# Gate stores on ScalarE, and one modulation pair with each gate, in a hybrid attention and mLSTM layer

## The chip, the cores and the metric

One Trainium2 chip, one core. The metric is device microseconds of one launch. TensorE is PE in the rows (PEld its weight load), VectorE DVE, ScalarE ACT, GpSimd POOL and SyncE SP. "The granted clock" is the share of TensorE's full 2.4 GHz that the chip granted in a stretch; 0.50 is 1.2 GHz.

## The reference, cut to what matters

One layer over 1,024 prompt rows and 64 sample rows (together T = 1,088 columns, all kept transposed), D_MODEL 1,024.

```python
mod = jax.nn.silu(c) @ w_ada + b_ada              # modulation, 6 x 1024 columns
sh1, sc1, g1, sh2, sc2, g2 = jnp.split(mod[:, None, :], 6, axis=-1)
u = _rmsnorm(x, norm1_g) * (1 + sc1) + sh1
sq, sk, sv, mqk_pre, mv, mo, mi, mf, ga, gb = jnp.split(u @ w_in, idx, axis=-1)
y_a = _stick_breaking(sq, k_all, v_all, q_start)  # 8 heads x 64
y_b = jax.nn.sigmoid(mo) * mlstm(mqk_pre, mv, mi, mf)
merged = jax.nn.sigmoid(ga) * (y_a @ w_a) + jax.nn.sigmoid(gb) * (y_b @ w_b)
x = x + g1 * (merged @ w_out)
u2 = _rmsnorm(x, norm2_g) * (1 + sc2) + sh2
x = x + g2 * ((jax.nn.silu(u2 @ w_ff_gate) * (u2 @ w_ff_up)) @ w_ff_down)
```

Two parts matter here. The gates ga and gb are needed only when the branches are merged, and the modulation from column block 16 on (g1, sh2, sc2, g2) only behind that; so both can be computed at any earlier time, as filling for TensorE.

## The kernel before, in words

Matrix products in f32 are made of three passes in a rounded format: each weight tile (128 columns of a weight matrix, 1,024 rows, 512 KB) is loaded by SP into a buffer `wr`, GpSimd splits it into a high part `wh` (L53) and a low part `wl` (L59), and `mm3` (L76, L77, L78) issues high x high, high x low and low x high. The pool `wp` has three buffers of each kind, used in turn.

The stretch of the program that the change touches has these units.

- A **gate unit** (`gate_unit`, 8 for ga and 8 for gb) loads one weight tile, runs 72 matmuls (3 chunks of 320, 384 and 384 columns, 24 each), takes the sigmoid of each chunk on ACT (L845) into a small tile `gt`, and stores it to a scratch tensor (L846). SP issues that store.
- A **modulation pair** (`ada_unit(i)`, blocks i and i+1; 16 of them are left for this stretch, in `ada_left`) loads two weight tiles `wada` of 512 KB each (L220) into two of the same three `wr` buffers, and has 32 small matmuls on PE (L223) and two transposes (L228).
- A **branch_b** step is one chunk of y_b @ w_b (12 matmuls into `ps_b`), of which there are 24 for 8 blocks and 3 chunks.
- An **attention pair** (`attention(p)`, p = 0 to 3, two heads each, and the sample group's rows) loads q, k and v from scratch by GpSimd (`load_head`, L454 to L457); per query tile PE makes the logits `z` (L546, L547), ACT two sigmoids `re` and `be` (L411, L412), DVE a running product from the right (L415) and a product (L416); then PE transposes (L560), ACT and DVE split the result (L47, L56), and PE multiplies by v (L567).

The fourth mLSTM head is emitted together with the first modulation pair and two gates. Then each of the first three attention pairs is emitted ahead of its filling: `run(attention(p), chain(gates_ada(ng, na)), 27, 0)` with four gates and three or four modulation pairs. The last pair is emitted up to its 14th step, then the filling that is left, then the rest of the pair, and then all of branch_b. What is written first has priority: the framework's scheduler plays the program against its own timeline and writes out a fixed order for each engine, in which work of later text fills the gaps of earlier text. On the chip each engine keeps to that order, and a DMA waits in its engine's queue until its data and its buffer are there. Behind this stretch, from about 900 us on, come w_a, w_out and the FFN.

Of the kernel before, what the change touches and what calls it, by code (L numbers as in the profile page):

```python
# [35 lines left out]
def trunk(ctx, tc, a, o, dbg=None, stop=None):  # L36
    nc = tc.nc
# [126 lines left out]
    def sum_step(x, k, c, when):  # L164

        nc.sync.dma_start(wsum_d[x][0:1, c, HC : HC + 1], when())
        src = sum_parts[x][k]
        src = wsum_d[src][:, c, :] if isinstance(src, int) else wpart(*src, c)
        if k:
            nc.gpsimd.dma_start(wsum_d[x][:, c, :], src, accum_op=ALU.add)  # L170
        else:
            nc.gpsimd.dma_start(wsum_d[x][:, c, :], src)
        return
        yield
# [7 lines left out]
    def small(shape, name, tag, dtype=F32, bufs=2, pool=None):  # L182
        return (pool or cur["sb"]).tile(shape, dtype, tag=tag, name=name, bufs=bufs)
# [170 lines left out]
    def unit(name, fills, evac, alloc=None, last=False):  # L354

        wh, wl = w_unit(fills, name)
        if alloc:
            alloc()
        for c, (s, e) in enumerate(CHUNKS):
            if last and c:  # L360
                break
            ps = bank("d", f"ps_{name}_{c}", cur["d"])
            for kb in range(KB):
                mm3(ps[:, : e - s], wh[:, kb, :], wl[:, kb, :], uh[kb][:, s:e], ul[kb][:, s:e], kb == 0, kb == KB - 1)
            evac(ps, s, e)
            yield
        if last:
            pss = [bank("d", f"ps_{name}_{c}", cur["d"]) for c in (1, 2)]
            for kb in range(KB):
                for ps, (s, e) in zip(pss, CHUNKS[1:]):  # L370
                    mm3(ps[:, : e - s], wh[:, kb, :], wl[:, kb, :], uh[kb][:, s:e], ul[kb][:, s:e], kb == 0, kb == KB - 1)
            for ps, (s, e) in zip(pss, CHUNKS[1:]):
                evac(ps, s, e)
            yield

    def w_cols(c0):
        return lambda raw: [(raw, cols(w_in, c0))]
# [464 lines left out]
    def gate_unit(b, c0, dst, name):  # L842
        def fin(ps, s, e):
            t = small([P, 384], f"gt_{name}{b}_{s}", "gt", bufs=cur["gt"])
            nc.scalar.activation(t[:, : e - s], ps[:, : e - s], AF.Sigmoid)  # L845
            nc.sync.dma_start(dst[b][:, s:e], t[:, : e - s])  # L846
        return unit(f"{name}{b}", w_cols(c0 + b * P), fin, None, name == "gb" and b == KB - 1)

    def in_unit(name, c0, i, evac, alloc):
        return unit(name, w_cols(c0), lambda ps, s, e: evac(*i, ps, s, e), lambda: alloc(*i))  # L850

    def qkv_units(p):
        return [in_unit(f"q{p}", OFF_Q + P * p, (p, 0), evac_qk, alloc_qk),
                in_unit(f"k{p}", OFF_K + P * p, (p, 1), evac_qk, alloc_qk), k_post(p),
                in_unit(f"v{p}", OFF_V + P * p, (p,), evac_v, alloc_v), v_post(p)]

    def ml_units(h):
        return [in_unit(f"mq{h}", OFF_MQ + P * h, (h, 0), evac_x, alloc_x),
                in_unit(f"mk{h}", OFF_MK + P * h, (h, 1), evac_x, alloc_x),
                in_unit(f"mv{h}", OFF_MV + P * h, (h,), evac_mv, alloc_mv),  # L860
                in_unit(f"mo{h}", OFF_MO + P * h, (h,), evac_mo, alloc_mo)]

    def ada_unit(i):

        ada_blocks((i, i + 1), "d", cur["d"], lambda i: wp.tile([P, KB, P], F32, tag="wr", name=f"wada{i}"))
        if i % 8 == 6:
            ada_bias(i - 6, 8)
        if i == 38:
            nc.vector.scalar_tensor_tensor(A2, mod[:, 32:40, :], 1.0, c1T[:, 48:56, None].to_broadcast([P, 8, 2]), ALU.add, ALU.mult)
        yield  # L870

    def chain(gens):
        for g in gens:
            yield from g

    def run(consumer, dense, nsteps, nd):

        n = 0.0
        done = False
        if nd == 0:  # L880
            for _ in consumer:
                pass
            done = True
        for _ in dense:
            n += nsteps / max(nd, 1)
            while n >= 1.0 and not done:
                n -= 1.0
                done = next(consumer, "end") == "end"
        for _ in consumer:
            pass  # L890

    gates = [gate_unit(b, OFF_GA, ga_d, "ga") for b in range(KB)] + [gate_unit(b, OFF_GB, gb_d, "gb") for b in range(KB)]
    ada_left = [ada_unit(i) for i in range(16, 48, 2)]
# [55 lines left out]
    sums = [(x, k, c) for x, k in ((1, 0), (3, 0), (1, 1), (2, 0), (2, 1), (3, 1), (4, 0), (4, 1)) for c in range(2)]  # L949
    for h in range(4):  # L950
        q_, k_, kp, v_, vp = qkv_units(h)
        m_ = ml_units(h + 1) if h < 3 else ada_left[0:1] + gates[0:2]
        def last(t):
            return t[0:1, T - 1 : T]

        said = [None, lambda h=h: last(pairs[h].kf), None, lambda h=h: last(pairs[h].vf), None]
        if h < 3:
            said += [lambda h=h: cvo[0:1, h + 1 : h + 2], lambda h=h: cvo[0:1, h + 5 : h + 6],
                     lambda h=h: last(heads[h + 1].vf), lambda h=h: last(heads[h + 1].og)]
        dense = []  # L960
        for i, g in enumerate([q_, k_, kp, v_, vp] + m_):
            dense.append(g)
            if i < len(said) and said[i] and sums:
                dense.append(sum_step(*sums.pop(0), said[i]))
        run(mlstm(h), chain(dense), 14, 23 if h < 3 else 17)
# [64 lines left out]
                nc.sync.dma_start(pb_d[m][:, s:e], t)  # L1030
                yield

    gi, ai = 2, 1

    def gates_ada(ng, na):
        nonlocal gi, ai
        gs, ads = gates[gi : gi + ng], ada_left[ai : ai + na]
        gi, ai = gi + ng, ai + na
        fill = []
        for i in range(ng):  # L1040
            fill += gs[i : i + 1] + ads[i : i + 1]
        return fill + ads[ng:]

    for p, (ng, na) in enumerate(((4, 3), (4, 4), (4, 4))):
        run(attention(p), chain(gates_ada(ng, na)), 27, 0)

    last_pair = attention(3)
    for _ in range(14):
        next(last_pair)
    for _ in chain(ada_left[ai : ai + 2] + gates[gi : gi + 1] + ada_left[ai + 2 :] + gates[gi + 1 :]):  # L1050
        pass
    wb0 = wide_unit(w_b, 0, 4, 0, "wb0")
    for b in range(4, 8):
# [39 lines left out]
    for m4 in range(0, KB, 4):  # L1093
# [3 lines left out]
        for c, m in [(c, m4 + i) for c in range(3) for i in range(4)]:  # L1097
# [12 lines left out]
            for lo, hi in ([(s, HT), (HT, e)] if s < HT < e else [(s, e)]):  # L1110
                h = lo // HT
# [668 lines left out]
```

## Time and profile before

| what | value |
|---|---|
| runs | 1782.4, 1779.88 and 1782.68 us, median 1782.4 |
| the profiled execution | 1784.58 us, of which its span is 1782.9 us |
| mean granted clock | 0.984 |
| PE busy | 1718.2 us (96%) |
| DVE, ACT, POOL busy | 1030.9, 747.8, 537.1 us (58%, 42%, 30%) |
| first and last gate store | 459.2 and 810.6 us |

The attention pairs lie between about 500 and 898 us. Busy shares are means over stages with different limits, so a change in this stretch is read from windows of it: the idle time of PE in a window, and beside it what PE's work lost by a granted clock under 1 (busy time times what the clock lacks to 1).

### The profile page before, as it was taken

What the parts mean: (1) busy time and instruction counts of PE and PEld (TensorE: products, weight loads), DVE (VectorE), ACT (ScalarE), POOL (GpSimd) and SP (SyncE); (2) the same over time, 40 slices, a digit from 0 to 9 for tenths busy, and PEclk for the clock granted to TensorE, in tenths of its full rate; (3) what the DMA queues carried; (4) which work ended last, traced back from release to release, by engine and by line L of the source; (5) the groups of instructions that cost most, each with busy time, mean ns of one, the idle gap of its engine ahead of it and who ended that gap; (6) DMA issues with size and microseconds to landing.
All of it is one profiled execution on the core that took longest, in us unless ns stands there. A gap on an engine that the chain in (4) does not pass through costs nothing. (4 is left out here: it accounts for less than half of the span.)

```text
span 1782.9 us, 32711 instructions
## 1 busy us (share of the span) xinstructions
PE 1718.2 (96%) x12670; PEld 1658.0 (93%) x12670; DVE 1030.9 (58%) x1962; ACT 747.8 (42%) x1513; POOL 537.1 (30%) x489
## 2 busy tenths in 40 slices
PE   6999999999989999789999999999999999999998
PEld 4899999999979998689899999999999999999998
DVE  5533325152244867576764389766555677667964
ACT  6333333324233535335533457533333345453444
POOL 1434544445433232143567240044322100000000
PEclk9999999999999999899999999999999999999999
DMA  9436666664485666767576355744433588899943
GB/s 274 116 99 209 146 193 143 187 162 138 136 203 150 160 167 151 167 157 244 170 217 191 99 147 166 197 145 166 137 99 98 163 231 240 299 338 356 289 134 101
DMA packets 361838, 320.24 MB, mean 180 GB/s; under 512 B 16983, under 2 KB 330835, under 8 KB 361683
## 3 DMA queue, kind: packets, MB, share of 16 engines
q1 hardware_dynamic: 347378, 270.77, 50.6%
q0 software_dynamic: 14304, 47.39, 10.8%
q8 instruction: 99, 1.62, 0.4%
q14 instruction: 57, 0.46, 0.1%
HBM read 241.01 MB, written 98.09 MB: 190 GB/s over the span
## 5 line engine op out<-in xcount | busy, mean ns | idle before, releaser
L1662 PE MATMUL ps_d<-o,wh_d 128*128 128x272 f32 x1232 | 230.8, 287 | 0.0
L1662 PEld LDWEIGHTS ps_d<-o,wh_d 128*128 128x128 f32 x1232 | 192.8, 188 | 0.0
L1662 PE MATMUL ps_d<-o,wl_d 128*128 128x272 f32 x616 | 176.4, 288 | 0.0
L1662 PEld LDWEIGHTS ps_d<-o,wl_d 128*128 128x128 f32 x616 | 115.5, 188 | 0.0
L47 ACT CAST w<-wr 128x512 fp32r<-128x512 f32 x140 | 84.6, 619 | 68.1 <-DMA wr<-in_w_ff_gate 17.5
L56 DVE TENSOR_TENSOR w<-wr,w 128x512 fp32r<-128x512 f32 x140 | 95.7, 696 | 22.5 <-ACT w L47 20.0
L415 DVE TENSOR_TENSOR_SCAN re<-re 128x128 f32<-128x128 f32 (+3 forms) x64 | 95.4, 1494 | 11.8 <-ACT re L411 11.5
L411 ACT ACTIVATE re<-z 128x512 f32<-128x512 f32 (+2 forms) x96 | 47.6, 496 | 90.3 <-DVE z L407 61.0
L1646 POOL DMA_DIRECT2D dsum_d<-wr_d x12 | 6.5, 538 | 237.4 <-DVE wr_d L1644 232.7
L1435 PE MATMUL ps_ga<-b1h,w 128*128 128x272 f32 x352 | 74.6, 289 | 3.1 <-ACT g L1420 2.0
L1435 PE MATMUL ps_gc<-b5h,w 128*128 128x272 f32 x352 | 75.2, 293 | 0.3 <-DVE g L1423 0.3
L1435 PE MATMUL ps_gd<-b4h,w 128*128 128x272 f32 x352 | 73.9, 290 | 1.3 <-DVE hst L1417 1.3
L1435 PE MATMUL ps_gd<-b7h,w 128*128 128x272 f32 x352 | 74.2, 290 | 0.1
L1435 PE MATMUL ps_gb<-b6h,w 128*128 128x272 f32 x352 | 74.3, 289 | 0.0
L1435 PE MATMUL ps_ga<-b2h,w 128*128 128x272 f32 x352 | 73.8, 288 | 0.0
L1435 PE MATMUL ps_gc<-b3h,w 128*128 128x272 f32 x352 | 73.7, 289 | 0.0
L76 PE MATMUL ps_gb<-uh,wh_gb 128*128 128x384 f32 (+1 forms) x192 | 65.9, 343 | 6.0 <-POOL wh_gb L53 5.2
L47 ACT CAST o<-hr 128x544 fp32r<-128x544 f32 x77 | 49.3, 645 | 51.9 <-DMA hr<-h_d 25.3
L47 ACT CAST wh_d<-wr_d 128x1024 fp32r<-128x1024 f32 (+1 forms) x42 | 41.1, 980 | 69.9 <-PE ps_d L1662 41.0
L76 PE MATMUL ps_ga<-uh,wh_ga 128*128 128x384 f32 (+1 forms) x192 | 65.2, 340 | 2.4 <-POOL wh_ga L53 1.2
L78 PE MATMUL ps_ga<-uh,wl_ga 128*128 128x384 f32 (+1 forms) x192 | 63.9, 333 | 2.6 <-POOL wl_ga L59 2.6
L56 DVE TENSOR_TENSOR o<-hr,o 128x544 fp32r<-128x544 f32 x77 | 53.9, 722 | 20.3 <-ACT o L47 20.0
(560 smaller groups left out, 5840.6 us busy)
## 6 DMA issues: line engine op xcount, KB each, us to landing
wada<-in_w_ada SPq DMA_DIRECT2D x48, 512.0 KB
wr<-wsum_d SPq DMA_DIRECT2D x80, 256.0 KB
wr_d<-in_w_ff_down SPq DMA_DIRECT2D x34, 512.0 KB
h_d<-hst SPq DMA_DIRECT2D x44, 272.0 KB
wr<-in_w_ff_gate SPq DMA_DIRECT2D x40, 256.0 KB
hr<-h_d SPq DMA_DIRECT2D x33, 272.0 KB
wsum_d<-in_w_ff_up POOLq DMA_DIRECT2D x6, 1282.0 KB, 7.7
wsum_d<-in_w_ff_gate POOLq DMA_DIRECT2D x6, 1282.0 KB, 7.9
```

Of the source, the lines that this page charges most:

```text
L47: nc.scalar.copy(out, in_)
L56: nc.vector.tensor_sub(out, in_, h.bitcast(F32))
L76: nc.tensor.matmul(ps, wh, xh, start=first, stop=False)
L78: nc.tensor.matmul(ps, wl, xh, start=False, stop=last)
L411: nc.scalar.activation(rest[:, c0 : c0 + w], ps, AF.Sigmoid, scale=-scale)
L415: nc.vector.tensor_tensor_scan(r, r, r, 1.0, ALU.mult, ALU.bypass)
L1435: nc.tensor.matmul(ps, w[:, a, j, :], b[j // 2][:, j % 2, :], start=p in (1, 6, 5, 7) and j == 0 and k == 0, stop=j == 3 and k == 2, skip_ ...
L1646: nc.gpsimd.dma_start(dsum_d[p][mp, ks[0] // 4][:, : P * n], flat)
L1662: nc.tensor.matmul(ps, a[:, j, mi, :], b[:, h], start=p not in (2, 4) and k == ks[0] and i == 0, stop=k == ks[-1] and i == 2, skip_group_c ...
```

## The change

The gate's store is issued by ACT, right behind the sigmoid whose tile it stores, and no longer by SP. The order of the filling is another: ahead of each gate stands one modulation pair. Before, the sequence on PE is a16 ga0 ga1 | ga2 a18 ga3 a20 ga4 a22 ga5 | ga6 a24 ga7 a26 gb0 a28 gb1 a30 | gb2 a32 gb3 a34 gb4 a36 gb5 a38 | a40 a42 gb6 a44 a46 gb7 (bars where a new attention pair's filling begins in the text); with the change a16 ga0 a18 ga1 | a28 ga2 a20 ga3 a22 ga4 a24 ga5 a26 | ga6 a30 ga7 a32 gb0 a34 gb1 a36 | gb2 a38 gb3 a40 gb4 a42 gb5 a44 | gb6 a46 gb7. All units are the same in number and content.

```diff
--- before.py
+++ after.py
@@ -843,7 +843,8 @@
         def fin(ps, s, e):
             t = small([P, 384], f"gt_{name}{b}_{s}", "gt", bufs=cur["gt"])
             nc.scalar.activation(t[:, : e - s], ps[:, : e - s], AF.Sigmoid)
-            nc.sync.dma_start(dst[b][:, s:e], t[:, : e - s])
+
+            nc.scalar.dma_start(dst[b][:, s:e], t[:, : e - s])
         return unit(f"{name}{b}", w_cols(c0 + b * P), fin, None, name == "gb" and b == KB - 1)
 
     def in_unit(name, c0, i, evac, alloc):
@@ -949,7 +950,7 @@
     sums = [(x, k, c) for x, k in ((1, 0), (3, 0), (1, 1), (2, 0), (2, 1), (3, 1), (4, 0), (4, 1)) for c in range(2)]
     for h in range(4):
         q_, k_, kp, v_, vp = qkv_units(h)
-        m_ = ml_units(h + 1) if h < 3 else ada_left[0:1] + gates[0:2]
+        m_ = ml_units(h + 1) if h < 3 else [ada_left[0], gates[0], ada_left[1], gates[1]]
         def last(t):
             return t[0:1, T - 1 : T]
 
@@ -1030,24 +1031,24 @@
                 nc.sync.dma_start(pb_d[m][:, s:e], t)
                 yield
 
-    gi, ai = 2, 1
+    gi, ai = 2, 2
 
     def gates_ada(ng, na):
         nonlocal gi, ai
         gs, ads = gates[gi : gi + ng], ada_left[ai : ai + na]
         gi, ai = gi + ng, ai + na
-        fill = []
-        for i in range(ng):
-            fill += gs[i : i + 1] + ads[i : i + 1]
-        return fill + ads[ng:]
-
-    for p, (ng, na) in enumerate(((4, 3), (4, 4), (4, 4))):
+        fill = ads[ng:]
+        for g, ad in zip(gs, ads):
+            fill += [g, ad]
+        return fill
+
+    for p, (ng, na) in enumerate(((4, 5), (4, 4), (4, 4))):
         run(attention(p), chain(gates_ada(ng, na)), 27, 0)
 
     last_pair = attention(3)
     for _ in range(14):
         next(last_pair)
-    for _ in chain(ada_left[ai : ai + 2] + gates[gi : gi + 1] + ada_left[ai + 2 :] + gates[gi + 1 :]):
+    for _ in chain([gates[gi], ada_left[ai], gates[gi + 1]]):
         pass
     wb0 = wide_unit(w_b, 0, 4, 0, "wb0")
     for b in range(4, 8):
```
The change has one line more in `gate_unit` (an empty one), so its line numbers behind it are higher by one: the store is L847.

Three places of the program show what it moves. The first is **SP's queue ahead of the last attention pair's filling**, with the modulation loads (`wada`, the number is the block) and the gates' loads (`wr_gb`). Before:

```order
L220 DMA wada39_8025<-in_w_ada 128x8x128
L220 DMA wada40_8398<-in_w_ada 128x8x128
L846 DMA gb_d_97<-gt_gb5_0_7955 128x320
L846 DMA gb_d_97<-gt_gb5_320_7983 128x384
L846 DMA gb_d_97<-gt_gb5_704_8011 128x384
L220 DMA wada41_8408<-in_w_ada 128x8x128
L220 DMA wada42_8424<-in_w_ada 128x8x128
L220 DMA wada43_8434<-in_w_ada 128x8x128
L467 DMA craw_v3_8065<-in_cache_sb_v 128x4x128
L64 DMA wr_gb6_8449<-in_w_in 128x8x128
L220 DMA wada44_8540<-in_w_ada 128x8x128
```
With the change:

```order
L220 DMA wada42_7979<-in_w_ada 128x8x128
L220 DMA wada43_7989<-in_w_ada 128x8x128
L64 DMA wr_gb5_8004<-in_w_in 128x8x128
L220 DMA wada44_8095<-in_w_ada 128x8x128
L585 DMA ya_d_94<-ya1_6006 128x1088
L220 DMA wada45_8105<-in_w_ada 128x8x128
L64 DMA wr_gb6_8475<-in_w_in 128x8x128
L220 DMA wada46_8566<-in_w_ada 128x8x128
L220 DMA wada47_8576<-in_w_ada 128x8x128
L64 DMA wr_gb7_8592<-in_w_in 128x8x128
```
Before, three modulation loads stand in a row behind the stores, and three more behind the load for gb6; with the change two loads and one gate's load alternate, and no gate store stands between them.

The second is **GpSimd's order at the start of the first attention pair**: the splits of gates 2 and 3, the fourth mLSTM head's output (`ybs`) and the loads of the first head (`qs`, `kh`, `kl`). Before:

```order
L53 TENSOR_SCALAR wh_ga3_5578<-wr_ga3_5576 128x1024
L59 TENSOR_TENSOR wl_ga3_5579<-wr_ga3_5576,wh_ga3_5578 128x1024
L812 TENSOR_TENSOR hsq3_4708<-hn3_4191 128x1152
L53 TENSOR_SCALAR ybs3_0_4770<-yb3_4754 128x1088
L59 TENSOR_TENSOR ybs3_1_4773<-yb3_4754,ybs3_0_4770 128x1088
L454 DMA qs0_0_4854<-qk_d_178 64x1088
L455 DMA kh0_0_4855<-qk_d_178 64x1088
L456 DMA kl0_0_4856<-qk_d_178 64x1088
```
With the change:

```order
L53 TENSOR_SCALAR wh_ga2_5514<-wr_ga2_5512 128x1024
L59 TENSOR_TENSOR wl_ga2_5515<-wr_ga2_5512,wh_ga2_5514 128x1024
L53 TENSOR_SCALAR ybs3_0_4762<-yb3_4746 128x1088
L59 TENSOR_TENSOR ybs3_1_4765<-yb3_4746,ybs3_0_4762 128x1088
L53 TENSOR_SCALAR wh_ga3_5630<-wr_ga3_5628 128x1024
L59 TENSOR_TENSOR wl_ga3_5631<-wr_ga3_5628,wh_ga3_5630 128x1024
L454 DMA qs0_0_4880<-qk_d_178 64x1088
L455 DMA kh0_0_4881<-qk_d_178 64x1088
L456 DMA kl0_0_4882<-qk_d_178 64x1088
```
Gate 3's two splits stood ahead of `ybs`; they now stand between `ybs` and the first head's loads.

The third is **PE's order at the start of the last head's long chain** (`z3_1_6` and `z3_1_7` are the logits of the last two query tiles; that head takes its tiles from the back). Before:

```order
L499 MATMUL z0s3_8339<-ckl3_8330,zq_4852 128x512
L546 MATMUL z3_1_6_512_8709<-kh3_1_8054,qs3_1_8053 128x384
L547 MATMUL z3_1_6_512_8709<-kl3_1_8055,qs3_1_8053 128x384
L76 MATMUL ps_b4_1_9332<-yh4_8688,wh_wb4_9236 128x384
L77 MATMUL ps_b4_1_9332<-yl4_8689,wh_wb4_9236 128x384
L78 MATMUL ps_b4_1_9332<-yh4_8688,wl_wb4_9237 128x384
L76 MATMUL ps_b4_1_9332<-yh5_8690,wh_wb4_9236 128x384
```
With the change:

```order
L546 MATMUL z3_1_6_0_8706<-kh3_1_8132,qs3_1_8131 128x512
L547 MATMUL z3_1_6_0_8706<-kl3_1_8133,qs3_1_8131 128x512
L77 MATMUL ps_b7_2_9465<-yl7_8695,wh_wb6_9242 128x384
L78 MATMUL ps_b7_2_9465<-yh7_8694,wl_wb6_9243 128x384
L546 MATMUL z3_1_6_512_8709<-kh3_1_8132,qs3_1_8131 128x384
L547 MATMUL z3_1_6_512_8709<-kl3_1_8133,qs3_1_8131 128x384
L506 MATMUL ps_as3_8439<-ident_66,be_s3_8430 128x128 x4
L509 MATMUL ps_as23_8448<-ident_66,be_s3_8430 64x128
L546 MATMUL z3_1_7_0_8722<-kh3_1_8132,qs3_1_8131 128x512
L547 MATMUL z3_1_7_0_8722<-kl3_1_8133,qs3_1_8131 128x512
```
Before, branch_b's steps `ps_b4_1` to `ps_b7_1` and `ps_b4_2` to `ps_b7_2` stand behind `z3_1_6_512`, between the steps of the chain; with the change all of branch_b stands ahead of it.

## Rows read from the trace of the kernel before

**Rows 1.** Page, part 1: engine, busy time, share of the span, instructions.

```profile
PE 1718.2 (96%) x12670; PEld 1658.0 (93%) x12670; DVE 1030.9 (58%) x1962; ACT 747.8 (42%) x1513; POOL 537.1 (30%) x489
```

**Rows 2.** Windows (start:end | length, busy us and instructions per engine, granted clock, DMA share, GB/s).

```profile
560.00:735.00 175.00, 171.75 (x1297) 158.40 (x1297) 121.26 (x221) 83.86 (x193) 46.89 (x52) 1.00 0.61 155
735.00:740.00 5.00, 2.22 (x30) 1.89 (x30) 1.07 (x5) 1.52 (x3) 0.58 (x1) 1.00 0.97 269
740.00:760.00 20.00, 12.44 (x77) 8.44 (x66) 9.90 (x28) 5.05 (x13) 7.08 (x8) 0.50 0.92 188
760.00:780.00 20.00, 20.00 (x162) 18.15 (x160) 11.99 (x20) 8.32 (x21) 3.01 (x4) 0.99 0.41 116
780.00:800.00 20.00, 15.34 (x101) 13.75 (x100) 19.89 (x26) 6.83 (x17) 15.89 (x12) 0.91 0.88 210
```

**Rows 3.** Timeline of PE, 735 to 763 us (start, length, engine, line, operation [idle before <- releaser]).

```profile
739.72 0.77 PE L223 MATMUL ps_ada<-wada,cT 128*32 128x128 f32 x16 [2.78 <-DMA wada<-in_w_ada]
...
745.78 1.08 PE L223 MATMUL ps_ada<-wada,cT 128*32 128x128 f32 x16 [2.36 <-DMA wada<-in_w_ada]
...
756.38 0.63 PE L76 MATMUL ps_gb<-uh,wh_gb 128*128 128x320 f32 x1 [4.65 <-POOL wh_gb L53]
```

**Rows 4.** Timeline of SP's queue, 712 to 760 us.

```profile
722.66 9.81 SPq L846 DMA_DIRECT2D gb_d<-gt_gb  x3
734.33 3.52 SPq L220 DMA_DIRECT2D wada<-in_w_ada  x3
...
743.48 15.69 SPq L220 DMA_DIRECT2D wada<-in_w_ada  x3
```

**Rows 5.** Waits of SP's queue, whole span: who is waited for, us in total, times, longest.

```profile
SPq L846 <- ACT gt_gb L845: 88.1, 21, 8.2
...
SPq L846 <- ACT gt_ga L845: 53.3, 15, 6.5
```

**Rows 6.** Line 846: instructions of it (ns min/median/max, first and last start).

```profile
L846 SPq DMA_DIRECT2D gb_d<-gt_gb x24: 319/338/339, 609.3 to 810.6; - x24
```

**Rows 7.** Windows, around the start of the first attention pair.

```profile
480.00:560.00 80.00, 73.96 (x522) 68.36 (x521) 35.72 (x69) 26.26 (x58) 31.56 (x31) 0.96 0.71 169
515.00:520.00 5.00, 2.62 (x23) 1.31 (x20) 2.78 (x6) 1.53 (x4) 2.78 (x3) 0.82 0.29 92
520.00:525.00 5.00, 3.15 (x12) 3.16 (x13) 1.67 (x3) 0.66 (x2) 1.79 (x1) 0.50 0.68 206
```

**Rows 8.** Timeline of POOL, 483 to 503 us.

```profile
487.88 0.60 POOL L454 DMA_DIRECT2D qs<-qk_d  x1
```

**Rows 9.** DMA issues, 485 to 505 us: xcount, KB each, median us to landing.

```profile
kl<-qk_d POOLq DMA_DIRECT2D x4, 272.0 KB, 11.6
```

**Rows 10.** Timeline of PE, 497 to 503 us.

```profile
500.98 0.40 PE L546 MATMUL z<-kh,qs 128*128 128x128 f32 x2
```

**Rows 11.** Timeline of POOL, 514 to 545 us.

```profile
519.46 2.33 POOL L59 TENSOR_TENSOR wl_ga<-wr_ga,wh_ga 128x1024 fp32r<-128x1024 f32 x1
...
539.11 1.05 POOL L53 TENSOR_SCALAR wh_ga<-wr_ga 128x1024 fp32r<-128x1024 f32 x1 [4.09 <-DMA wr_ga<-in_w_in]
```

**Rows 12.** Windows, the fill ahead of the last head's chain, and that chain.

```profile
820.00:855.00 35.00, 33.71 (x220) 32.56 (x219) 16.34 (x25) 18.35 (x39) 18.05 (x16) 1.00 0.60 192
855.70:897.70 42.00, 37.70 (x221) 34.08 (x221) 37.49 (x57) 24.60 (x57) 24.80 (x20) 0.96 0.51 164
882.00:897.70 15.70, 12.70 (x85) 10.42 (x84) 13.71 (x27) 10.29 (x24) 7.58 (x11) 1.00 0.66 219
```

**Rows 13.** Timeline of PE, 854 to 862 us.

```profile
855.93 0.33 PE L77 MATMUL ps_b<-yl,wh_wb 128*128 128x384 f32 x1
...
857.67 0.33 PE L78 MATMUL ps_b<-yh,wl_wb 128*128 128x384 f32 x1
```

**Rows 14.** Timeline of DVE, 855 to 900 us.

```profile
855.97 0.30 DVE L407 TENSOR_TENSOR z<-z,amask 128x128 f32<-128x128 f32 x1 [6.13 <-PE z L547]
...
897.77 0.62 DVE L56 TENSOR_TENSOR yl<-ya,yh 128x320 fp32r<-128x320 f32 x1 [0.53 <-ACT yh L47]
```

## The prediction

> **What bounds the kernel now.** I read the page's engine shares first: PE is busy 96% of the span [rows 1], so a change pays only where it fills a hole of PE or gives its clock back. The windows come next, because the mean hides where the holes are. From 560 to 735 us, where gates and modulation pairs alternate one for one, PE is idle 175.00 − 171.75 = 3.25 us at full clock, 1.9% [rows 2]. In the next 65 us, where the last pairs stand bunched (a38, a40, a42, then one gate, then a44, a46), idle time is 2.78 + 7.56 + 0 + 4.66 = 15.0 us, and the granted clock falls to 0.50 for 20 us and to 0.91 for another 20: busy time times the missing clock is 12.44 × 0.50 + 20.00 × 0.01 + 15.34 × 0.09 = 7.8 us [rows 2]. That is 22.8 us lost in 65. The timeline of PE names what it waited for: twice a modulation load, then the split of gate gb6's weights [rows 3]. SP's timeline shows those loads one behind the other, the last three drawn out over 15.69 us, with stores that held the queue for 9.81 us ahead of them [rows 4], and the DMA engines are over 0.9 busy for the 25 us from 735 us on [rows 2]. A pair brings 1 MB for some 2 us of PE work; bunched, it starves PE, spread it does not.
>
> **The change, part by part.**
>
> *1. The bunch is dissolved (gain).* The same 65 us at the rate of the stretch before would lose 65 × 1.9% = 1.2 us, so 22.8 − 1.2 = **−21.6 us**. Upper end: all of it, −22.8. Lower end: 780 to 800 us has DVE busy 19.89 of 20 us [rows 2], so its loss of 4.66 + 1.4 = 6.1 us may be the attention chain's own, which leaves −15.5. I take −21.6, because DVE was held up by the starved PE just before (9.90 of 20 us busy) and was catching up.
>
> *2. The first attention pair starts later (cost).* Gate 3's load now stands on SP behind wada21, whose buffer comes free only when PE has done pair a28, and its splits stand on GpSimd ahead of the first head's loads. Those loads began at 487.88 us [rows 8], they take a median of 11.6 us from issue to landing [rows 9], and the first logits ran at 500.98 [rows 10]: 13.1 us from the first load to the first logits, nearly all of it loading. With the change a28 comes right behind gate 1 and the mLSTM's last transposes, at about 487 us as I count PE's order; three weight tiles then queue, of which one alone took 4.09 us from free buffer to landed [rows 11]. I put gate 3's at 493, its splits (1.05 + 2.33 us, [rows 11]) at 497, the head loads at 498, the first logits at 498 + 13 = 511 us. PE arrives there at about 500 (487 plus gate 2's 72 matmuls of 0.17 us), so it stands for about 10 us; the matmuls behind run at half clock for a few us, as they did behind the stall at 520 us [rows 7], 2.5 us; and 0.5 more for what follows. That is 13 us. What the stretch loses now goes with it: 480 to 560 us has 6.04 us idle and 2.62 × 0.18 + 3.15 × 0.50 = 2.1 us of clock [rows 7], 8.1 in all, most of it waits on splits that moved ahead. Net **+4.9 us**. Ends: −2 (the head loads hide behind gate 2 and half of today's waits go) and +13 (both stay).
>
> *3. The last head's chain loses its cover (cost).* In the trace PE works on branch_b while the last head's chain goes through ACT and DVE. DVE waited 6.13 us for PE's logits at 855.97 and ends at 898.4 [rows 14]; until then PE set the time, with 33.71 of 35 us busy [rows 12]. Behind these logits stand 8 steps of branch_b, 8 × 12 = 96 matmuls at (857.67 − 855.93) / 10 = 0.174 us [rows 13], 16.7 us. The change puts them all ahead of the logits: PE reaches them **+16.7 us** later. The chain behind is then freed of them. It took 42.0 us with DVE busy 37.49 and PE 37.70 [rows 12]; PE keeps 37.7 − 16.7 = 21.0 us, so DVE's own 37.5 us is the bound: **−4.5 us**. Ends for the bare chain: 32 us (the sample rows' scan and product move ahead, and GpSimd's 24.80 us of products, which ran beside DVE, mostly too) and 50 us (rival B). Net +12.2.
>
> *4. The stores change queue.* SP's queue waited 88.1 + 53.3 = 141 us for sigmoids [rows 5]; that goes. It pays nothing by itself, since PE was idle only 3.25 us in the 175 us with the most of these waits; this is the end on the side of gain, −3.3. ACT issues 48 stores more, 48 × 0.338 = 16.2 us [rows 6], over some 350 us in which it was busy 83.86 of 175, or 48% [rows 2]. A store waits for nothing on ACT but the sigmoid just ahead. Queued behind it are the next sigmoids of attention, and DVE waits for those; if that cover were gone, a fifth of the 16.2 us would show, +3. I take **0**. The Trainium skill (DMA: Bandwidth & Descriptors, "Issuing engines are not separate DMA queues") says that DMAs issued by different engines run on the same 16 DMA engines, and that spreading them saves only the issue time. By it the end of −3.3 falls away and the sum stays.
>
> w_a, w_out and the FFN stay as they are: 0.
>
> Sum: −21.6 + 4.9 + 12.2 + 0 = **−4.5 us**. The sum is made against the profiled execution, 1784.58 us, which gives 1780.1. That execution lies 2.2 us above the median of the runs, so against 1782.4 the forecast is **1777.9 us**. No measurement of this kernel can tell less than about 0.2%, 3.6 us, from no change.
>
> **The rivals.**
>
> *A, no measurable change.* The loss only moves: the stall at the first pair takes its upper end of +13, or the gain its lower end of −15.5, while the chain costs its +12.2. The first gives −21.6 + 13 + 12.2 = +3.6, the second −15.5 + 4.9 + 12.2 = +1.6; both with some luck elsewhere lie within 3.6 us of zero: about 1782. For it: the bytes and the matmuls are the same. Against it: the bunch is the largest hole of the stretch.
>
> *B, slower: the bare chain lasts longer.* Without branch_b, PE has 21.0 us of work in the chain in many short pieces between waits on ACT and DVE. In the trace the granted clock was 0.50 where PE was busy 12.44 of 20 us with small pieces [rows 2], and 1.00 where it was busy 12.70 of 15.7 at the chain's end [rows 12]. If the clock falls, PE's part takes up to 42 us and stands in series with ACT and DVE. The point from which it decides is a chain of 42.0 + 4.5 − 0.9 = 45.6 us: there the sum becomes −21.6 + 4.9 + 16.7 + 3.6 = +3.6. At 50 us it is +8.0, **1790 us**. The Trainium skill (TensorE: Matmul & The Clock Gate, Part 1) states that the throttled state is the default and that activity releases it; by that rule the sparse chain falls to 1.2 GHz. The two stretches named show one of each.
>
> *C, a larger gain.* The chain shrinks to 32 us and the start costs nothing: −21.6 − 2 + 16.7 − 10 = −16.9, **1765.5 us**. For it: DVE's work shares its time with GpSimd's products now. Against it: PE, ACT and DVE wait for each other in the chain.
>
> *D, the change does only the stores' part*, if the order on the chip were not what moves the time: 0 from part 4, inside A.
>
> **How the numbers follow.** Forecast, between −3.6 and −10 us: 0.38. A with D: 0.28. B, with the start's stall at its upper end counted in: 0.24. C and what lies between it and the forecast: 0.10. Faster is then 0.38 + 0.10 = 0.48, the same 0.28, slower 0.24. For 8 in 10 the range takes in most of C and of B: **1766 to 1790 us**; the likeliest case's own range is 1772 to 1779.
>
> **What would show it.** Step 1: the windows of the stretch that holds gb5 to gb7 show PE over 97% busy at a clock of 1.00, and no wait on `wada` above 1 us. Step 2: PE waits about 10 us for the first head's loads near 500 us; without that wait the step is wrong. Step 3: no `ps_b` matmul behind `z3_1_6_512`, and 37 to 38 us from there to the last `yl`; the granted clock in it tells B. Step 4: no store of gates on SP, and DVE's waits on ACT's `re` no longer than before. The forecast is wrong if new waits on `wada` appear where a28 was pulled ahead, or if the chain is over 45.6 us.

## The result and the profile after

The changed kernel takes 1791.93 us in the median of four runs (1790.43 to 1794.98), the kernel before 1782.54 us. The ratio is 1.0057, 95% interval [1.004, 1.0075], that is +10.2 us (7.1 to 13.4). It is slower, above the range of 1766 to 1790, where 4.5 us less was forecast. The profiled execution, the longest of the four, has a span of 1793.3 us against 1782.9 us before.

The windows of the changed kernel, cut at the same places of the program as far as that is possible (columns as in [rows 2]; 870.08 us is the last head's `z3_1_6_512`, 906.93 us the end of the last `yl`):

```profile
480.00:560.00 80.00, 69.61 (x514) 64.40 (x513) 36.20 (x70) 23.43 (x53) 29.48 (x31) 0.91 0.76 188
560.00:735.00 175.00, 169.66 (x1254) 154.82 (x1253) 119.62 (x219) 80.31 (x187) 55.04 (x54) 0.99 0.64 159
735.00:800.00 65.00, 62.21 (x441) 58.92 (x440) 40.11 (x64) 27.11 (x63) 27.56 (x23) 0.97 0.68 203
800.00:870.00 70.00, 65.01 (x405) 62.05 (x404) 41.95 (x67) 35.78 (x79) 36.25 (x32) 0.98 0.67 182
870.08:906.93 36.85, 25.57 (x129) 19.25 (x129) 34.19 (x60) 20.14 (x48) 22.70 (x20) 0.81 0.30 99
```

Idle time of PE plus what its work lost by a clock under 1 (here and below summed over windows of 5 us, since a mean clock over a long window also counts idle time). The last row is different: it gives the length of that part, with the 96 matmuls at the prediction's 16.7 us. In the kernel before it begins at 855.52 us, where this row is `z3_1_6_512`:

```profile
855.52 0.34 PE L547 MATMUL z<-kl,qs 128*128 128x384 f32 x1
```

| stretch | before | changed | difference | forecast |
|---|---|---|---|---|
| 480 to 560 us | 8.1 | 10.4 + 4.6 = 15.0 | +6.9 | +4.9 |
| 560 to 735 us | 3.3 | 5.3 + 1.4 = 6.7 | +3.4 | 0 |
| 735 to 800 us | 22.8 | 2.8 + 1.5 = 4.3 | −18.5 | −21.6 |
| 800 us to `z3_1_6_512` | 1.3 | 5.0 + 1.7 = 6.7 | +5.4 | 0 |
| the 96 `ps_b` matmuls ahead of it, and the chain behind | 42.9 | 16.7 + 36.9 = 53.6 | +10.7 | +12.2 |

The sum is +7.9; attention ends at 906.9 us against 898.4 us, 8.5 us later, and another 1.9 us come behind it. The bunch of modulation loads [rows 2, 3] is dissolved as forecast. Its 18.5 us, and 7.9 more, are spent again at the start, at the end, and in two stretches for which nothing was forecast. There PE no longer waits for loads but for attention's own chain and for branch_b's copies. The waits of PE from 560 to 735 us, and from 735 to 870 us (who, for whom: us in total, times, longest):

```profile
PE po L567 <- DVE al L56: 3.2, 2, 2.9
PE ps_a L560 <- DVE be L416: 2.1, 3, 1.1
```

```profile
PE ps_b L76 <- ACT tb L1029: 3.9, 3, 2.6
PE po_s L518 <- DVE al_s L56: 2.4, 1, 2.4
```

At the start (PE's, ACT's and POOL's timelines; compare [rows 8, 10]):

```profile
497.82 0.69 PE L76 MATMUL ps_ga<-uh,wh_ga 128*128 128x384 f32 x1 [7.35 <-ACT gt_ga L845]
...
511.58 0.76 PE L546 MATMUL z<-kh,qs 128*128 128x128 f32 x2 [3.05 <-DMA kh<-qk_d]
```

```profile
497.33 0.44 ACT L845 ACTIVATE gt_ga<-ps_ga 128x320 f32<-128x320 f32 x1 [12.67 <-DMA yb_d<-ybs]
```

```profile
499.35 0.60 POOL L454 DMA_DIRECT2D qs<-qk_d  x1
```

The head loads begin at 499.35 us and the first logits at 511.58 us; 498 and 511 were forecast. But the larger wait stands ahead of them: gate 2's first sigmoid waits for the store of the mLSTM's output `yb_d`, and PE waits for the sigmoid, since its two accumulator banks still hold chunks that have not been read. The sigmoid neither reads nor writes `yb`. In the program its small tile `gt` is among the first of a new group of buffers, opened right behind the closing of the group that held `ybs`; so the wait is, as far as the program tells, for that memory. No run gave the tile another place.

### The profile page after: what moved, and what is told of

Its sections match the earlier page's. It is cut to its first block, busy times and chain, and to the rows that moved or that the text cites. A ratio compares the mean times of both kernels' runs of the same rounds, so it can differ in the third digit from the quotient of the medians.

```text
span 1793.3 us, 32659 instructions
## 1 busy us (share of the span) xinstructions
PE 1722.3 (96%) x12670; PEld 1661.3 (93%) x12670; DVE 1032.5 (58%) x1962; ACT 746.2 (42%) x1513; POOL 546.4 (30%) x489
## 5 line engine op out<-in xcount | busy, mean ns | idle before, releaser
L47 ACT CAST w<-wr 128x512 fp32r<-128x512 f32 x140 | 84.5, 619 | 69.1 <-PE ps_gc L1436 18.5
L415 DVE TENSOR_TENSOR_SCAN re<-re 128x128 f32<-128x128 f32 (+3 forms) x64 | 95.4, 1494 | 15.3 <-ACT re L411 14.8
L56 DVE TENSOR_TENSOR al<-ps_a,ah 128x512 fp32r<-128x512 f32 (+1 forms) x80 | 49.8, 631 | 32.0 <-ACT ah L47 31.5
L56 DVE TENSOR_TENSOR o<-hr,o 128x544 fp32r<-128x544 f32 x77 | 54.0, 722 | 21.2 <-ACT o L47 20.8
```

The costliest lines, as they stand in the source:

```text
L47: nc.scalar.copy(out, in_)
L56: nc.vector.tensor_sub(out, in_, h.bitcast(F32))
L415: nc.vector.tensor_tensor_scan(r, r, r, 1.0, ALU.mult, ALU.bypass)
```

## The experiments

All ratios are to the kernel before, timed beside each run on the same chip (e1 to e4 on one chip, e5 to e8, e9 to e11 and e12 to e15 each on another); 0.1% is 1.8 us. Single executions of one kernel lie several us apart, so a trace need not show a median execution; where this matters it is said. Line numbers in rows are those of each run's own kernel.

### e1 and e2: the two halves of the change

e1 is the kernel before with L846's `nc.sync` made `nc.scalar`; e2 is the changed kernel with its L847 set back to `nc.sync`.

> The order of the kernel before, with only the gate stores moved to ACT; PE's order is that of before, 96 branch_b matmuls still behind the last head's logits. Theory (the time is made by the order of the filling: first pair's start +6.9, bare end +10.7, new waits of PE on DVE and ACT +8.9, bunch dissolved -18.6): no change, within 3.6 us of 1782.5. Rival 1 (the new waits of PE on DVE and ACT come from the 48 stores that ACT now issues): +5 to +9 us. Rival 2 (SP freed of 141 us of waiting brings the bunched loads forward): -5 us or more, with less than half of the 22.8 us lost at the bunch.

> The changed order with the stores still on SP. Theory (order makes the time): like the changed kernel within 3.6 us, so 1788 to 1796, with PE's 7 us wait on the first sigmoid of gate 2 near 490 us and a bare end of 36 to 38 us. Rival 1 (ACT's stores make the new waits of 8.9 us): 1783. Rival 2 (stores on SP hold up the alternating loads): over 1797.

Stores alone: 1.0021 [1.0004, 1.0038], +3.7 us. Order alone: 1.0084 [1.006, 1.0109], +15 us. So the loss is the order's. The stores on ACT cost a little in the old order; in the new order the changed kernel stands lower than e2, on the side of e2's rival 2, though the intervals overlap; e8 below decides it. Freeing SP did not dissolve the bunch: e1 still loses 11.4 + 6.9 = 18.3 us from 735 to 800 us (in an execution 6 us above its median).

### e3 and e4: the start as before

```diff
-        m_ = ml_units(h + 1) if h < 3 else [ada_left[0], gates[0], ada_left[1], gates[1]]
+        m_ = ml_units(h + 1) if h < 3 else ada_left[0:1] + gates[0:2]
...
-    for p, (ng, na) in enumerate(((4, 5), (4, 4), (4, 4))):
+    for p, (ng, na) in enumerate(((4, 4), (4, 4), (4, 4))):
...
-    for _ in chain([gates[gi], ada_left[ai], gates[gi + 1]]):
+    for _ in chain([ada_left[ai], gates[gi], ada_left[ai + 1], gates[gi + 1], ada_left[ai + 2]]):
```

That is e3 (with `gi, ai = 2, 1`). e4 keeps the changed `m_`, has (4, 4) in place of (4, 5), and a46 behind the last gate.

> Stores on ACT and one pair ahead of each gate, but the fourth mLSTM head keeps its filling of before (one pair, two gates), so gate 3's split stands ahead of ybs again, and 84 branch_b matmuls stay behind the last head's logits (before 96, changed 0). Theory (the costs add up): the start's +6.9 and nearly all of the end's +10.7 go, so 1774 to 1778. Rival (spread pairs only trade the bunch for waits along the whole stretch, the order of attention being what PE waits for): 1781 or more.

> The changed kernel without pair a28 pulled ahead of gate 2: gate 3's split stands ahead of ybs as before, but all of branch_b still stands ahead of the last head's logits (0 behind). Theory (costs add up): only the start's +6.9 goes, 1783 to 1787. Rival 1 (the late start of attention is what makes the whole loss, the bare end included): 1779 or less. Rival 2 (the start costs nothing in the end, since attention catches up where PE is not the bound): 1790 to 1793.

e3: 0.9996 [0.998, 1.0012], e4: 1.0057 [1.0036, 1.0079]. e3 is no faster than before, so its theory's 1774 to 1778 us was missed. Yet it is lower than e1, which has the same stores: 0.9996 / 1.0021 gives −0.25%, some 4.5 us for spread pairs where start and end are nearly kept. The two intervals overlap a little; the means of their 12 executions each, timed together, lie 5.3 us apart. In its trace, of an execution 6 us under its median, 735 to 800 us loses 7.8 + 3.4 = 11.2 us. In e4 the start is repaired (9.1 us lost from 480 to 560 us in place of 15.0) and the time is the changed kernel's: the next stretch loses 12.1 us in place of 6.7. Rival 2 of e4 holds.

### e5 to e8: the end

An order edge on PE, and nothing else (e5 on the changed kernel, e7 on e4, e8 on e2):

```diff
+                        if (p, i, t, k0) == (3, 1, 6, 512):
+                            mark.append(zi.ins)
...
+                with tc.issue_after(mark[0]) if m4 and c else ExitStack():
+                    for k in range(4):
+                        mm3(ps[:, :n], wh[:, k, m % 2, :], wl[:, k, m % 2, :], yh[4 + k][:, s:e], yl[4 + k][:, s:e], k == 0, k == 3)
```

e6 does the reverse in the kernel before:

```diff
+                if m4 and c:
+                    pb = next(x for x in reversed(nc.cur_bb.bb.instructions) if x.engine == mark[0].engine)
+                    tc.add_manual_dep(mark[0], pb.name, mybir.DependencyInfo(
+                        mybir.DependencyClass.NoSync, mybir.DependencyReason.DATA), reason="bare")
```

> The changed kernel with one thing more: the 8 branch_b steps (96 matmuls) that the kernel before has behind the last head's logits z3_1_6_512 are ordered behind them again, by an order edge on PE; PE's order up to there is the changed kernel's. Theory (the bare end is what makes the changed kernel slower, +10.7 by the windows): the ratio to before falls from 1.0057 to between 0.998 and 1.001, and the stretch from these logits to the last yl takes 41 to 44 us. Rival (cover only lengthens the chain by its own 16.7 us, and the spread pairs are what costs): still 1.004 or more.

> The kernel before with one thing changed: the 96 branch_b matmuls behind z3_1_6_512 are ordered ahead of it. Theory (bare end costs 10.7 us whatever the filling's order): 1.005 to 1.007 of before, the chain 36 to 38 us long and starting 16 to 17 us later, at a granted clock near 0.82. Rival (the end costs nothing, the order of the filling does): within 0.2% of before.

> Run e4 (start repaired) with the 96 matmuls behind the last head's logits as in e5. Theory (once the end is covered, the start's 6.9 us count): 5 to 7 us less than e5, 0.994 to 0.998 of before. Rival (e4 showed it: what the start saves is given back as waits on attention's chain from 560 us on): like e5 within 0.2%.

> Run e2 (changed order, stores on SP) with the 96 matmuls behind the last head's logits as in e5. Theory (with pairs and gates alternating, stores that hold SP's queue cost some 5 us, as e2 against the changed kernel): 3 to 6 us more than e5. Rival (the stores' queue is worth nothing once the end is covered): like e5 within 0.2%.

e6: 1.0094 [1.0071, 1.0117], +16.8 us (12.6 to 20.8), more than expected. Its chain, after `z3_1_6_512` at 874.72 us (before 855.52):

```profile
874.72:910.72 36.00, 26.26 (x113) 20.76 (x113) 32.83 (x53) 18.17 (x42) 21.20 (x21) 0.72 0.32 107
```

PE is idle 9.7 of 36 us and the granted clock is 0.72, a mean over stretches at 0.50 and at 1.00, where the covered chain had 0.96 [rows 12]. So a bare end is dear in the old order. But e5 is 1.0052 [1.0032, 1.0072], e7 1.005 [1.0031, 1.0068] and e8 1.008 [1.0058, 1.0103]: in the new order, moving these 96 matmuls behind the logits gives back nothing measurable, with the start repaired or not (compare the changed kernel's 1.0057, e4's 1.0057 and e2's 1.0084). The trace of e5 shows PE at `z3_1_6_512` 13 us sooner, and waiting ahead of it instead:

```profile
800.00:857.00 57.00, 49.64 (x276) 45.01 (x276) 38.16 (x59) 30.48 (x69) 22.88 (x17) 0.87 0.55 160
857.08:898.72 41.64, 38.77 (x226) 35.78 (x226) 36.23 (x61) 24.75 (x56) 19.17 (x17) 0.94 0.42 133
```

Without these 96 matmuls 800 to 857 us is idle 7.4 us at a clock of 0.87. (This execution, 1784.8 us, is 5 us under e5's median.) The costs do not add up.

e8's theory held: beside e5, from which it differs in the stores' queue alone, it is 5.5 us slower in the median (five executions at 1792.0 to 1796.9 us, six of e5 at 1784.8 to 1792.9). So in the new order the stores on ACT are worth some 5 us, where in the order of before they cost a little. A part of it can be seen: in e8's trace PE waits, from 735 to 875 us, for branch_b's loads of `yb_d`, which SP issues behind gate stores.

```profile
PE ps_b L77 <- DMA yl<-yb_d: 2.0, 2, 1.7
```

e2's trace has 2.9 us of such waits, for `yl` and `yh`; those of e5 and of the changed kernel have none. Where the rest of the 5 us goes is not shown.

### e11: the bunch alone

```diff
-    for _ in chain(ada_left[ai : ai + 2] + gates[gi : gi + 1] + ada_left[ai + 2 :] + gates[gi + 1 :]):
+    for _ in chain([ada_left[ai], gates[gi], ada_left[ai + 1], gates[gi + 1], ada_left[ai + 2], ada_left[ai + 3]]):
```

> The kernel before with only the last filling in another order, a40 gb6 a42 gb7 a44 a46 in place of a40 a42 gb6 a44 a46 gb7; stores on SP, start and first three pairs as before, 156 branch_b matmuls behind the last head's logits. Theory of the prediction (the 22.9 us lost at the bunch are a loss that spreading gives back, if start and end keep what they have): 0.989 to 0.995 of before. Rival (the holes at the bunch were time in which attention's chain on ACT and DVE caught up, so PE waits for DVE elsewhere instead): 0.997 to 1.002.

1.0012 [0.9997, 1.0027]: no gain from an edit that the theory priced at 9 to 20 us.

```profile
735.00:800.00 65.00, 58.73 (x463) 52.29 (x462) 43.62 (x85) 27.23 (x65) 17.01 (x21) 0.92 0.71 170
800.00:855.00 55.00, 44.42 (x269) 41.17 (x268) 31.66 (x48) 25.55 (x55) 22.94 (x17) 0.84 0.65 206
```

The first stretch loses 9.8 us in place of 22.8; the second 16.4 in place of 1.3, partly on a46's load (6.1 us), partly on DVE (4.5 us). The hole moved by 60 us. This is no clean test of spreading: a44 and a46 still stand in a row, and the longest wait is for the second of them.

### e9, e10, e12 to e15: the heads' loads

In the traces of the slower orders the loads of a pair's second head stand on GpSimd behind the splits of a gate whose weights come late. e12 puts the kernel before into that state at one place; the others take it out, by edges of the form

```diff
+        with tc.issue_after(hl[pins[name]]) if pins.get(name) in hl else ExitStack():
+            wh, wl = w_unit(fills, name)
...
+        hl[p, i] = nc.gpsimd.dma_start(vs, v_d[p, i, :, 1:9]).ins
```

with `pins` {ga3: (0, 1), gb0: (1, 1)} in e9, on the changed kernel; {gb0: (1, 1)} in e10, on e3; {gb0: (1, 1), gb5: (2, 1)} in e13, on e4, and in e15, on e3; {ga3: (0, 1), ga7: (1, 1), gb0: (1, 1), gb4: (2, 1)} in e14, on the changed kernel. In e12 the six q and k loads of head (2, 1) get an edge from gb5's second split.

> The changed kernel with two order edges on GpSimd and nothing else: the splits of gate ga3 stand behind both heads' loads of the first attention pair, those of gb0 behind the second head's loads of the second pair. With these edges the framework's scheduler by itself leaves 84 branch_b matmuls behind the last head's logits (changed kernel 0, before 96). Theory (head loads that queue on GpSimd behind the split of a late weight load delay the whole attention chain; the bare end and PE's waits on DVE follow from that): PE's wait for the first loads near 510 us and DVE's waits of 5 to 7 us for qs go, ratio 0.997 to 1.001 against 1.0057 of the changed kernel. Rival (one pair ahead of each gate costs by itself, e5 and e7 having moved nothing): 1.004 or more.

> Run e3 with the splits of gb0 behind the second head's loads of the second pair, as in e9; 144 branch_b matmuls are then behind the last head's logits. Theory (late head loads are what is left of the cost in e3): DVE's wait of 4.4 us for qs near 607 us goes, 2 to 5 us less than e3, 0.996 to 0.999 of before. Rival (e3 has no such cost left; PE's holes only move): 0.999 or more.

> The kernel before with one order edge on GpSimd: q, k of the third pair's second head are loaded behind the splits of gate gb5 (before: ahead of them). All else as before, 96 branch_b matmuls stay behind the last head's logits. Theory (late head loads delay attention's chain): these loads are issued some 18 us later (at about 702 in place of 683.65 us), DVE waits for qs 5 us or more there, PE waits on DVE behind it, 1.002 to 1.005 of before. Rival (attention has slack there): within 0.1% of before.

> Run e4 with two order edges on GpSimd: the splits of gb0 behind the loads of the second pair's second head, those of gb5 behind the loads of the third pair's second head. 84 branch_b matmuls are then behind the last head's logits by themselves (e4: 0). Theory (late head loads are what makes e4 slow, since e7 showed that the bare end alone does not): DVE's waits of 5.3 and 6.2 us for qs go, PE's loss from 560 to 735 us falls from 12 to under 5 us, 0.997 to 1.001 against 1.0057. Rival (pairs ahead of each gate cost by themselves): 1.004 or more.

> The changed kernel with four order edges on GpSimd, so that no split of a late weight load stands ahead of head loads: ga3 behind the first pair's loads, ga7 and gb0 behind those of the second pair's second head, gb4 behind those of the third pair's. (e9 had two of them, and ga7's split took gb0's place ahead of the loads.) 144 branch_b matmuls are behind the last head's logits. Theory: DVE waits under 2 us for qs at each pair, 0.997 to 1.001 of before; what then stays is PE's wait of 7 to 9 us on gate 2's first sigmoid near 490 us. Rival: 1.004 or more as e9.

> Run e3 with the edges of e13 (e10 had only that for gb0, and the split of gb5 moved ahead of the third pair's vs load, where DVE waited 6.8 us for qs). 144 branch_b matmuls behind the last head's logits. Theory (spread pairs with loads on time and a covered end): the best of all, 0.994 to 0.999. Rival (nothing is left to gain in e3): 0.999 to 1.002.

e12: 1.0025 [1.001, 1.004], +4.5 us (1.8 to 7.1) for one late load. POOL's, DVE's and PE's timelines:

```profile
696.87 1.06 POOL L53 TENSOR_SCALAR wh_gb<-wr_gb 128x1024 fp32r<-128x1024 f32 x1 [18.86 <-DMA wr_gb<-in_w_in]
698.02 2.92 POOL L59 TENSOR_TENSOR wl_gb<-wr_gb,wh_gb 128x1024 fp32r<-128x1024 f32 x1
700.88 0.58 POOL L462 DMA_DIRECT2D qs<-qk_d  x1
```

```profile
711.39 0.20 DVE L505 CAST zq<-qs 128x64 fp32r<-128x64 f32 x1 [6.04 <-DMA qs<-qk_d]
```

```profile
712.10 0.58 PE L577 MATMUL po<-al,vs 128*128 128x256 f32 x1 [2.65 <-DVE re L418]
```

In the trace of the kernel before, the same loads are issued from 683.65 us on and DVE waits 1.24 us. A load that sits behind a split waiting 18.86 us for other data holds up DVE, and DVE holds up PE: that much is shown. The price is that of the runs' times. The trace, of an execution at the median, accounts for less: PE loses 5.0 us from 560 to 735 us in place of 3.3, and attention ends 1.3 us later than before.

e13: 1.0013 [1.0, 1.0025] against e4's 1.0057, −0.44% for two edges and the 84 matmuls that the scheduler then leaves behind the logits. The expected sign did not come, though: 560 to 735 us still loses 8.5 + 4.0 = 12.5 us, and DVE still waits 7.15 us for `qs` near 702 us, because the load, issued at 690.34 us where e4 has 702.35, still lands later than DVE is ready:

```profile
702.13 0.20 DVE L499 CAST zq<-qs 128x64 fp32r<-128x64 f32 x1 [7.15 <-DMA qs<-qk_d]
```

What fell is the end, which the scheduler covers again: `z3_1_6_512` stands at 856.44 us and attention ends at 898.2 us (e4: 867.35 and 904.9). So cover was worth something here, and the finding of e5, e7 and e8 holds for the edge that moves 96 matmuls alone: e7, with the same start, loses 12.4 us from 800 to 855 us, e13 5.9 us.

e9 is 1.0041 [1.002, 1.0062] and e14 1.004 [1.0018, 1.0061]: little or nothing against the changed kernel. In e9's trace ga7's split took gb0's place ahead of the loads and DVE still waits 6.1 us for `qs`; in e14's it waits 6.9 and 4.2 us, where its theory wanted under 2. e14's mean hides two groups of executions: seven at 1780.8 to 1786.5 us, within the spread of the kernel before (1777.2 to 1787.1), and five at 1790.7 to 1797.2. e10, 1.0039 [1.0024, 1.0054], and e15, 1.0045 [1.0029, 1.0061], are slower than e3. There the theory fails: with the edges DVE waits 6.8 and 7.1 us for `qs` near 701 us where e3 waited 0.8.

### e16 and e17: two kernels again

> The kernel of e9 once more, for the trace of a usual execution: e9's profile shows one of 1781.9 us, but 10 of its 12 executions took 1791 to 1799 us. Theory (the order leaves PE dependent on when loads land, and a late landing costs twice, as idle time and as half clock): 1791 to 1798 us, with 8 to 14 us more of idle time and missing clock than e9's profile, in waits of PE on DVE or on loads between 560 and 900 us. Rival (the difference lies behind 900 us, outside the changed stretch): the chain of attention ends at 895 to 897 us as in e9's profile.

> The kernel of e5 once more, for the trace of a usual execution: e5's profile shows one of 1784.8 us, the other five took 1789 to 1793 us. Theory: 1789 to 1793 us with 4 to 8 us more of idle time and missing clock between 480 and 900 us. Rival (the difference lies behind 900 us): attention ends at 898 to 899 us as in e5's profile.

e9's executions form two groups as well, two of twelve near 1782 us and ten at 1791 to 1799. e16, the same kernel, took 1788.5 us, under the expected 1791 to 1798, but shows where such a difference can lie. PE's wait on gate 2's first sigmoid in e9 and in e16, and what the sigmoid waited for in e16:

```profile
499.46 0.69 PE L76 MATMUL ps_ga<-uh,wh_ga 128*128 128x384 f32 x1 [8.93 <-ACT gt_ga L849]
```

```profile
512.78 0.69 PE L76 MATMUL ps_ga<-uh,wh_ga 128*128 128x384 f32 x1 [23.16 <-ACT gt_ga L849]
```

```profile
512.29 0.44 ACT L849 ACTIVATE gt_ga<-ps_ga 128x320 f32<-128x320 f32 x1 [28.48 <-DMA yb_d<-ybs]
```

The store of `yb_d`, issued at 490.25 and 490.15 us, released the sigmoid, and with it PE, 13 us apart; attention ends at 896.1 and 906.4 us. The difference lies in the changed stretch, but at the start and not where it was expected. e17, 1787.0 us where 1789 to 1793 were expected, with attention's end at 901.0 us, lies between e5's trace and its median.

## Why the prediction was wrong

**What bounds the kernel** was read by PE's idle time alone, and here the mistake begins. From 560 us on attention's chain (logits, ACT, DVE, transposes) runs beside PE with little slack. That the bunch was also the time in which this chain caught up fits DVE's 19.89 of 20 us [rows 2] and e11's waits on DVE, but no run isolates it.

**Step 1** is the one that failed. In its own stretch it was nearly right: 18.5 us came back, 3.1 less than forecast, though PE was busy 62.21 of 65 us (96%) where over 97% was named as the sign. But the term took the stretch "at the rate of the stretch before" and put its neighbours at nothing, and they lost 3.4 + 5.4 = 8.8 us more. Net −9.7 us in place of −21.6, in the trace. In place of the loads PE waited for DVE's `al` and `be` (5.3 us, 560 to 735 us) and for branch_b's copies and `al_s` (6.3 us, 735 to 870 us). Measured with start and end nearly kept (e3 against e1) the step is some −4.5 us; in e11, which spreads the last filling in part, it is nothing. The lower end, −15.5 us, was still too hopeful. It left out that a wait of PE that goes uncovers the next one.

**Step 2** was right in its mechanism and 2 us small: loads at 499.35 us, logits at 511.58, PE idle 10.4 us where about 10 were forecast. That the idle time fits is in part luck. The prediction had no wait on the store of `yb_d`; it takes 7.35 us, ahead of the loads' wait and in most of its place, and only 3.05 us were left of the latter. In e9 the head loads are issued at 490.17 us and PE still waits 8.93 us for that store. The wait comes with pair a28: every trace with it ahead of gate 2 has it, no other (table in the last section). In the time, repairing the start alone pays nothing (e4, and e7 against e5).

**Step 3** was right: no `ps_b` behind `z3_1_6_512`, the chain 36.85 us long where 37.5 were forecast, +10.7 in place of +12.2 us. e6 prices it alone, in the order of before, at 16.8 us. Of rival B only the clock came true: 0.81 in this chain and 0.72 in e6's, with PE busy 25.57 of 36.85 and 26.26 of 36.00 us. The rule of the Trainium skill (TensorE: Matmul & The Clock Gate, Part 1) that the throttled state is the default and activity releases it agrees with these two windows against the covered chain's 0.96. The chain was no longer for the lower clock: DVE was busy for 34.19 of its 36.85 us.

**Step 4** took 0, and that holds for neither order. In the order of before, the stores on ACT cost 3.7 us (e1, 0.7 to 6.8), a little over the upper end of +3, and the bunch stayed, so SP's waits were worth nothing there, as forecast. In the new order they gain some 5 us (e5 against e8, and the changed kernel against e2), beyond the end of −3.3; the forecast had priced SP's queue by PE's idle time in the order of before. So the order alone costs 15 us (e2), and the stores gave a third of it back. DVE's waits for `re`, named as the sign of a cost on ACT, grew from 11.5 to 14.8 us, but e2, with the stores on SP, has 17.2 and e1 9.7, so the traces put them on the order.

The sum by the trace's sizes, in which the stores' part is contained, is −9.7 + 6.9 + 10.7 = +7.9 us, and 1.9 us behind attention make nearly the whole +10.4 us of the two spans. The sign was wrong because of step 1: with −9.7 in place of −21.6 the forecast itself would have been +7.4 us. Rival A, that the loss only moves, was the nearest in its mechanism, though it kept within 3.6 us of zero; rival B's 1790 us was the nearest number, by a longer chain that did not come.

Open: why covering the end gives nothing in the new order when baring it costs 16.8 us in the old. The traces show the wait moving ahead of the logits (e5, e7) and less of it where the scheduler placed the cover itself (e13), not why its size is the same. No kernel tried is faster than the one before beyond its interval; e3 equals it.

## What to carry to other kernels

A hole of the bounding engine is not a gain waiting to be taken: ask which chain beside it may be catching up in that hole, and price the edit by the wait that comes next, not by the rate of a quiet neighbour. Where an engine's queue carries both loads and work that waits for other data, look in the order for a load that falls behind such work; one such place cost 4.5 us here. Price a queue in the order that it will stand in: the same move of the stores cost 3.7 us in the old order and gained some 5 in the new one. Where a long chain ends a stage, count what covers it before and after an edit that pulls filling forward: 96 matmuls of cover were worth 16.8 us here, though not in every order.

## What the runs showed of the hardware

The time from a store's issue until the engine that waited for its memory went on varied far more than expected: by 13 us between two executions of the same kernel (e9, e16). The store of `yb_d` ran there beside three loads on SP's queue, two of weights and one of the cache, and the heads' loads on GpSimd's. The Trainium skill (DMA: Bandwidth & Descriptors, "Issuing engines are not separate DMA queues") says that DMAs of all issuing engines share 16 DMA engines and interleave; that fits, but no run isolates it.

In the kernel before the head loads also began at 487.88 us, but gate 2's first sigmoid ran at 491.94 us and cost PE 1.2 us. What differs is the order on SP. In the changed kernel two weight loads are issued at 489.15 and 489.65 us, just ahead of the second of the two stores of `yb_d` at 490.41; in the kernel before that store is issued at 487.96 us, and no weight load from 480 to 497 us. The traces fall into three groups by it, by the time from that store's issue to the sigmoid:

| traces | two weight loads just ahead | head loads beside the store | store to sigmoid | wait of PE |
|---|---|---|---|---|
| before, e1, e3, e4, e6, e7, e10 to e13, e15 | no | yes | 4.0 to 4.1 us | 1.2 to 1.3 us |
| changed, e2, e5, e8, e17 | yes | no, later | 6.4 to 7.0 us | 6.6 to 8.0 us |
| e9, e14, e16 | yes | yes | 8.7, 12.2 and 22.1 us | 8.9, 12.7 and 23.2 us |

So a store behind two weight loads took longer than one without them in every trace, and longest where the heads' loads ran beside it too. The orders differ in other things as well, so no run isolates the loads as the cause.
